# A two-layer trunk step with S5 scan: scan tables and outputs kept on all 128 partitions, quarters of the scan interleaved

## The chip, the cores and the metric

The kernel runs on one core of a Trainium2 chip. The metric is the device time of one execution in microseconds (us), the median of several runs. Less is better.

## The reference

One step of a two-layer trunk over 128 context tokens and 512 latent tokens, all float32, model width 1024. Each layer is

```
h = modulate(x, shift1, scale1); z = h @ w_in
y_a, h_re, h_im = mixer_ssm(u_ssm, ...)      # scan: both directions
y_b = block_attention(q, k, v)               # MLA: q and kv from low-rank parts of z
y_c = mixer_gmlp(uv)
x = x + gate1 * (concat(rms(y_a), rms(y_b), rms(y_c)) * g @ w_out)
x = x + gate2 * conv_ffn(modulate(x, shift2, scale2))
```

and the scan, for each of 16 groups of 16 channels with 64 complex states, forward and reverse, is

```
a_bar = exp(A * dt); b_bar = (a_bar - 1) / A * B
bu    = einsum('gpc,blgc->blgp', b_bar, u)   # edge += a_bar * h0
h     = associative_scan(h = a*h + bu)
y     = einsum('gcp,blgp->blgc', C, h).real  # both directions added, + D * u
y     = gelu(y); y = y * sigmoid(y @ w_glu)
```

The final states of the context tokens (`new_ssm_re`, `new_ssm_im`) are outputs too.

## The kernel before

The scan is chunked: eight time steps become one column of `U` (81 columns `NC`, `NS` = 82 with a start column), so a group's 16 channels by 8 steps fill 128 rows, and a product with a precomputed 128-row table advances eight steps. The 16 groups are handled in four **quarters** of four groups: group `h * 8 + 2 * q + e`, with half `h` and `e` in 0, 1. `ssm_tables` (L530) builds, for each quarter, the tables `we` (input to state), `Q` (state to output) and `tap` (the part of the output that comes straight from the input); `ssm_rotations` (L648) builds the powers `Tr` that turn the complex recurrence into a real one. All go to DRAM (`WEd`, `Qd`, `Wd`, `Td`) and come back per quarter in `ssm_load` (as `we`, `qt`, `tp`, `T`), asked for on the POOL queue. In layer 0, DVE makes the tables of quarters 0 to 2 and POOL those of quarter 3 and the rotations, in front of and beside the input projection; layer 1's tables and rotations are made by POOL during layer 0's ConvFFN.

`ssm_quarter` (L701) does one quarter: 16 products `e` (L716) into two PSUM banks, copies `E` on ACT (L720), start states `h0` and zeros on POOL (L724 to L735), the rotation `m`, `E` on DVE (L744 to L747), the scan `H` (L752), the rotation back (L754, L755), the states `hq` by eight DVE instructions of 64 partitions (L761, L763), twelve products `y` (L775 to L777) into one bank, the copy `ys` (L779) and its way to DRAM (L781). A quarter's matrices hold real parts in rows 0 to 63 and imaginary parts in rows 64 to 127, so each product contracts 128 rows. `ssm_output` (L794) reads `yT` back, does gelu and the `glu` products; then attention begins (`mx`, L1248).

Every tile here has one buffer per tag, so a tile's next load or write waits for its last reader, and one tag may serve two tiles at different times: in layer 0 the rotations' `Tr` uses the memory of `hq`. Two PSUM banks (`pz`) serve `e`, `y` and `tap` in layer 0. The order of the instructions on each engine is not that of the code: a scheduler in the framework sets it when the kernel is built, and each engine then takes its queue strictly in that order. `params` (L166) loads small per-layer vectors; layer 1's are asked for in `mixers` of layer 0, after tables 0 to 2.

## Time and profile before

| | |
|---|---|
| median of 3 runs | 1826.63 us (1825.92 to 1826.67) |
| profiled execution | 1826.58 us, of which its span 1824.8 us and 1.78 us around it |
| TensorE (PE) busy | 1694.3 us, 93% of the span |
| VectorE (DVE) busy | 1156.8 us, 63% |
| ScalarE (ACT) busy | 679.8 us, 37% |
| GpSimd (POOL) busy | 312.8 us, 17% |
| mean granted TensorE clock | 0.95 |

The span of a layer divides into norm, tables and input projection, scan (about 149 to 213 us and 1018 to 1067 us), the rest of the mixers, attention, out projection and ConvFFN. Busy shares are means over stages that differ; the section of rows below gives stretches of 50 us and of 400 us, the waits by engine, and single instructions in order of time. PEclk is the granted clock as a share of full speed.

### The profile page before, as it was taken

To read this page: it belongs to the slowest core of one execution; us is meant where nothing else is said; L and a number is where in the kernel's file an instruction comes from. 1 tells how busy PE (TensorE), PEld (TensorE's weight loads), DVE (VectorE), ACT (ScalarE), POOL (GpSimd) and SP (SyncE) were. 2 spreads that over 40 slices of the span, in tenths; PEclk is the share of its full clock that TensorE was granted. 3 is DMA by queue.
4 is the path that set the end of the run, shared out by engine and by line. 5 is a ranking of instruction groups with operands and counts; after the bars stand their busy time and mean duration, and the time that the engine had idled before them with its cause. 6 is when DMAs were issued, how large, how long until landed. Compare 5 with 4: busy or idle time off the path is not lost.

```text
span 1824.8 us, 28970 instructions
## 1 busy us (share of the span) xinstructions
PE 1694.3 (93%) x11248; PEld 1512.6 (83%) x11248; DVE 1156.8 (63%) x2421; ACT 679.8 (37%) x1210; POOL 312.8 (17%) x738
## 2 busy tenths in 40 slices
PE   5878889999989999999999888999989999999998
PEld 3767755468889999999999876455989999999998
DVE  6887875667674646556477568566786464555564
ACT  4334454433452414224244346343344232332241
POOL 2886200000086060540000120000000000000000
PEclk7889789899899999999999978999989999999999
DMA  9265453301443523234132633540223131331221
GB/s 281 84 174 148 124 162 123 110 15 56 129 137 118 170 56 116 59 94 116 35 90 67 164 105 107 167 133 1 70 70 93 36 104 47 93 92 36 82 82 58
DMA packets 217577, 182.48 MB, mean 100 GB/s; under 512 B 33438, under 2 KB 202204, under 8 KB 217440
## 3 DMA queue, kind: packets, MB, share of 16 engines
q1 hardware_dynamic: 194736, 154.33, 28.2%
q0 software_dynamic: 8272, 23.87, 4.4%
q10 hardware_dynamic: 14432, 2.44, 0.7%
q8 instruction: 89, 1.46, 0.3%
q14 instruction: 48, 0.39, 0.1%
HBM read 161.94 MB, written 18.64 MB: 99 GB/s over the span
## 4 chain that ended last, share of the span: by engine, by line
PE 75%; DVE 10%; DMA 7%; ACT 4%; POOL 2%; issue 2%; ACTq 1%; SPq 0%; DVEq 0%; POOLq 0%
PE up L141 11%; PE up L143 11%; PE up L142 11%; PE dn L142 6%; PE dn L141 6%; PE dn L143 6%; PE o L1287 3%; PE mod L261 2%; DMA raw<-w_mod 2%; PE wo L141 1%; PE wo L143 1%; PE wo L142 1%; DMA raw<-ffn_w_up 1%; PE s L1267 1%; PE win L141 1%
## 5 line engine op out<-in xcount | busy, mean ns | idle before, releaser
L141 PE MATMUL up<-hh,whi 128*128 128x322 f32 x1408 | 435.6, 315 | 8.8 <-ACT hh L357 7.9
L143 PE MATMUL up<-hh,wlo 128*128 128x322 f32 x1408 | 440.9, 314 | 1.1 <-DVE wlo L118 1.0
L142 PE MATMUL up<-hl,whi 128*128 128x322 f32 x1408 | 439.7, 313 | 1.6 <-DVE hl L358 1.5
L141 PEld LDWEIGHTS up<-hh,whi 128*128 128x128 f32 x1408 | 266.1, 191 | 14.3 <-ACT hh L357 7.2
L142 PEld LDWEIGHTS up<-hl,whi 128*128 128x128 f32 x1408 | 268.8, 191 | 2.6 <-DVE hl L358 2.6
L143 PEld LDWEIGHTS up<-hh,wlo 128*128 128x128 f32 x1408 | 267.9, 190 | 2.9 <-DVE wlo L118 1.9
L118 DVE TENSOR_TENSOR wlo<-raw,whi 128x1024 fp32r<-128x1024 f32 (+1 forms) x116 | 146.7, 1266 | 142.2 <-ACT whi L117 141.0
L142 PE MATMUL dn<-glo,dh 128*128 128x322 f32 (+1 forms) x704 | 218.5, 312 | 0.2 <-DVE glo L118 0.2
L143 PE MATMUL dn<-gh,dl 128*128 128x322 f32 (+1 forms) x704 | 217.9, 311 | 0.0
L141 PE MATMUL dn<-gh,dh 128*128 128x322 f32 (+1 forms) x704 | 209.4, 312 | 4.5 <-DVE xT L1501 2.9
L1501 DVE SCALAR_TENSOR_TENSOR xT<-dn,mod,xT 128x320 f32<-128x320 f32 (+2 forms) x288 | 112.2, 435 | 129.5 <-PE dn L143 129.3
L117 ACT CAST whi<-raw 128x1024 fp32r<-128x1024 f32 (+1 forms) x116 | 120.5, 1040 | 151.1 <-PE up L142 56.8
L1532 ACT ACTIVATE cv<-up,prm,cw 128x321 f32<-128x321 f32 x88 | 54.3, 619 | 252.5 <-PE up L143 252.3
L141 PEld LDWEIGHTS dn<-gh,dh 128*128 128x128 f32 x704 | 131.0, 190 | 5.3 <-DVE xT L1501 3.1
L142 PEld LDWEIGHTS dn<-glo,dh 128*128 128x128 f32 x704 | 133.2, 189 | 0.5 <-DVE glo L118 0.5
L143 PEld LDWEIGHTS dn<-gh,dl 128*128 128x128 f32 x704 | 133.5, 190 | 0.0
L1533 DVE SCALAR_TENSOR_TENSOR cv<-up,cw,cv 128x320 f32<-128x320 f32 x88 | 48.3, 549 | 67.5 <-ACT cv L1532 67.5
L261 PE MATMUL mod<-raw,sT 128*32 128x256 f32 x768 | 64.5, 431 | 27.1 <-DMA raw<-w_mod 24.8
L118 DVE TENSOR_TENSOR dl<-raw,dh 128x1024 fp32r<-128x1024 f32 x44 | 54.0, 1227 | 45.8 <-ACT dh L117 45.6
L117 ACT CAST dh<-raw 128x1024 fp32r<-128x1024 f32 x44 | 46.1, 1047 | 56.8 <-DMA raw<-ffn_w_down 50.1
L261 PEld LDWEIGHTS mod<-raw,sT 128*32 128x32 f32 x768 | 19.5, 114 | 57.5 <-DMA raw<-w_mod 29.2
L1250 DVE TENSOR_REDUCE nml<-mx 128x1 f32<-128x640 f32 x64 | 50.9, 820 | 24.0 <-PE mx L1248 23.7
(472 smaller groups left out, 3422.5 us busy)
## 6 DMA issues: line engine op xcount, KB each, us to landing
raw<-w_mod SPq DMA_DIRECT2D x96, 512.0 KB, 4.6
raw<-ffn_w_up SPq DMA_DIRECT2D x88, 512.0 KB, 4.1
raw<-ffn_w_down SPq DMA_DIRECT2D x44, 512.0 KB, 3.5
raw<-w_in SPq DMA_DIRECT2D x10, 512.0 KB, 5.7
we<-WEd POOLq DMA_DIRECT2D x8, 512.0 KB, 4.1
qt<-Qd POOLq DMA_DIRECT2D x8, 512.0 KB, 5.1
raw<-w_out SPq DMA_DIRECT2D x16, 256.0 KB, 5.1
raw<-w_out SPq DMA_DIRECT2D x8, 512.0 KB, 3.4
```

The costliest lines, as they stand in the source:

```text
L117: self.nc.scalar.copy(hi, raw)
L118: self.nc.vector.tensor_tensor(lo, raw, hi.bitcast(F32), op=OP.subtract)
L141: mm(ps, wh, xh, start=start, stop=False)
L142: mm(ps, wh, xl, start=False, stop=False)
L143: mm(ps, wl, xh, start=False, stop=stop)
L261: nc.tensor.matmul(ps[j * 32:j * 32 + 32, c0:c0 + 256], self.sT[:, k0 + j, :], rv[:, j, :], start=k0 == 0, stop=k0 == 4)
L1250: V.tensor_reduce(nm[:, tt:tt + 1], pb[:, :, :320], axis=AX.XY, op=OP.max, negate=True)
L1267: mm(ps, kh[i][:, kc_], qh[i], start=True, stop=False)
L1287: mm(pb[i * 64:(i + 1) * 64, 0], Vt[:, kt, 2 * p + i], Ps[i][kt], start=kt == 0, stop=kt == 4)
L1501: self.nc.vector.scalar_tensor_tensor(self.xT[:, m, a:b], po[:, a - lo:b - lo], self.modcol(l, gi, m, c), self.xT[:, m, a:b], op0=OP.mult, ...
L1532: A.activation(z[:, 0:321], po[:, 0:321], AF.Identity, bias=b, scale=c1)
L1533: V.scalar_tensor_tensor(z[:, 1:321], po[:, 0:320], c0, z[:, 1:321], op0=OP.mult, op1=OP.add)
```

## The change

Scan tables and outputs stay on 128 partitions: the real and the imaginary part of both halves `h` lie in separate columns instead of separate rows. `hq` takes four instructions of 128 partitions in place of eight of 64, `Q` one subtract in place of two, and the copies `bs` go. The products that contracted 128 rows (real over imaginary) become two of 64 rows: `y` is 16 products of 64 rows and 4 of 128 in place of 12 of 128, `tap` 24 of 64 rows in place of 16 of 128, each `h` with its own PSUM bank, evacuated by two copies. The rotations are made in two halves that each serve two quarters in both directions, in layer 0 in the memory of `yA`, no longer of `hq`. The quarters become generators of three steps (load `we` and make `E`; load `T`, `qt`, `tp`; DVE and output), taken in the order 0 0 1 0 1 2 1 2 3 2 3 3. Quarter 0 of layer 1 is no longer loaded ahead of `uT`. The final states leave by eight DMAs a layer in place of two. Layer 1's parameters are asked for on the SP queue.

```diff
 def params(self, l):
+        q = nc.sync if l else nc.gpsimd
...
-                nc.gpsimd.dma_start(out=rows[r0:r1], in_=src)
-            nc.gpsimd.dma_start(out=rows[107:108, :96], in_=I["q_norm"][l:l + 1])
-            nc.gpsimd.dma_start(out=rows[108:109, :96], in_=I["k_norm"][l:l + 1])
+                q.dma_start(out=rows[r0:r1], in_=src)
+            q.dma_start(out=rows[107:108, :96], in_=I["q_norm"][l:l + 1])
+            q.dma_start(out=rows[108:109, :96], in_=I["k_norm"][l:l + 1])
...
+        def tap_of():
+            if not ps_of_:
+                return [self.pz("tap"), self.pz("tap")]
+            pb = self.pb("tap")
+            return [pb[:, 0], pb[:, 1]]
+
...
-        bb = t("bb", [128, 2, 2, 2, 16])
+        bbx = t("bb", [128, 144])
+        nc.gpsimd.memset(bbx[:, 128:], 0.0)
+        bb = bbx[:, :128].rearrange("p (r d g c) -> p r d g c", r=2, d=2, g=2)
...
-
-        bs = t("bs", [128, 2 * 64 + 16])
-        nc.gpsimd.memset(bs[:, 128:], 0.0)
-        for ri in range(2):
-            for h in range(2):
-                nc.scalar.copy(
-                    bs[ri * 64:(ri + 1) * 64, :128].rearrange("p (d h n) -> p d h n", d=2, h=2)[:, :, h],
-                    bb[h * 64:(h + 1) * 64, ri].rearrange("p d g c -> p d (g c)"))
...
-                for h in range(2):
-                    a = slice(h * 64, (h + 1) * 64)
-                    E.tensor_tensor(Q[part * 64:part * 64 + 64, h], tm[0][a], tm[1][a],
-                                    op=OP.subtract)
-            Qv = Q.rearrange("p h (g n) -> p h g n", g=2)
+                E.tensor_tensor(Q[:, part], tm[0], tm[1], op=OP.subtract)
+            Qv = Q.rearrange("p r (g n) -> p r g n", g=2)
...
-            for h in range(2):
-                put.dma_start(out=self.Qd[l][q][:, d, h], in_=Qv[:, h, :, o:o + 128])
+            for part in range(2):
+                put.dma_start(out=self.Qd[l][q][:, d, part], in_=Qv[:, part, :, o:o + 128])
...
-        ps = ps_of("tap")
-        for h in range(2):
-            for e in range(2):
+        ps = tap_of()
+        mm = nc.tensor.matmul
+        for e in range(2):
+            for h in range(2):
...
-                o = ps[gq * 32:gq * 32 + 32, :240]
-                lf = bs[:, gq * 16:gq * 16 + 32]
-                lb = bs[:, 64 + gq * 16:64 + gq * 16 + 32]
-                mm = nc.tensor.matmul
-                mm(o[:, 0:112], lb, Qs[1][:, h, e, 16:128], start=True, stop=True)
-                mm(o[:, 112:128], lb, Qs[1][:, h, e, 128:144], start=True, stop=False)
-                mm(o[:, 112:128], lf, Qs[0][:, h, e, 0:16], start=False, stop=True)
-                mm(o[:, 128:240], lf, Qs[0][:, h, e, 16:128], start=True, stop=True)
+            for o0, o1, d, n0 in ((0, 128, 1, 16), (112, 128, 0, 0), (128, 240, 0, 16)):
+                for r in range(2):
+                    for h in range(2):
+                        a, gq = slice(h * 64, h * 64 + 64), 2 * h + e
+                        c = r * 64 + d * 32 + e * 16
+                        mm(ps[h][gq * 32:gq * 32 + 32, o0:o1], bbx[a, c:c + 32],
+                           Qs[d][a, r, e, n0:n0 + o1 - o0], start=r == 0 and o0 != 112,
+                           stop=r == 1 and o0 != 0)
...
-        nc.scalar.copy(W, ps[:, :240])
+        for h in range(2):
+            nc.scalar.copy(W[h * 64:h * 64 + 64], ps[h][h * 64:h * 64 + 64, :240])
...
-    def ssm_rotations(self, l, pool, E, parts, tags=("Tr", "tr")):
+    def ssm_rotations(self, l, E, homes):
...
-            T = pool.tile([128, N, 2, NS], F32, name=self.uid("Tr"), tag=tags[0], bufs=1)
-            tm = pool.tile([128, 2, N * 32], F32, name=self.uid("tr"), tag=tags[1], bufs=1)
...
+        for a in range(2):
+            T = homes[0][0].tile([128, 2, 4, 2, NS], F32, name=self.uid("Tr"), tag=homes[0][1], bufs=1)
+            tm = homes[1][0].tile([128, 2, 8 * 32], F32, name=self.uid("tr"), tag=homes[1][1], bufs=1)
...
-                sh = [128, N, n]
...
-            for i in range(0, N, 2):
-                d, q = divmod(p0 + i, 8)
-                nc.gpsimd.dma_start(
...
+                sh = [128, 2, 4, n]
+                r_re, r_im = (bc(self.rho[:, j, r, l * 16:l * 16 + 16].rearrange(
+                    "p (d g) -> p d g", d=2)[:, :, 4 * a:4 * a + 4, None], sh) for r in range(2))
...
+            for q in range(2):
+                for d in range(2):
+                    nc.gpsimd.dma_start(
...
+        yield we
...
-        return we, T, qt, tp
-
-    def ssm_quarter(self, l, q, pool, tables, U, st, hq):
+        yield T, qt, tp
+
+    def ssm_quarter(self, l, q, pool, U, st):
...
-        we, T, qt, tp = tables
+        tables = self.ssm_load(l, q, pool)
+        we = next(tables)
...
+        yield
+        T, qt, tp = next(tables)
+        yield
+        hq = t("hq", [128, 2, 2, 2, NS])
+
...
+        for d in range(2):
+            sl = slice(0, 82) if d == 0 else slice(80, None, -1)
+            n = 82 if d == 0 else 81
+            V.tensor_tensor(hq[:, 0, d, :, 0:n], m1[:, d, :, 0, sl], m1[:, d, :, 1, sl],
+                            op=OP.subtract)
+            V.tensor_tensor(hq[:, 1, d, :, 0:n], m2[:, d, :, 0, sl], m2[:, d, :, 1, sl],
+                            op=OP.add)
+        for d in range(2):
+            nc.gpsimd.tensor_copy(st[:, :, d, 2 * q:2 * q + 2], hq[:, :, d, :, 81 if d == 0 else 64])
+        pv = [self.pz("y")[:, :2 * NC].rearrange("p (e k) -> p e k", e=2) for _ in range(2)]
+        for e in range(2):
+            for d in range(2):
+                for r in range(2):
+                    for h in range(2):
+                        a = slice(h * 64, h * 64 + 64)
+                        nc.tensor.matmul(pv[h][:, e], qt[a, d, r, e, :], hq[a, r, d, e, :NC],
+                                         start=d == 0 and r == 0, stop=False)
+            for h in range(2):
+                nc.tensor.matmul(pv[h][:, e], tp[:, h, e], U[:, h * 8 + 2 * q + e, :],
+                                 start=False, stop=True)
+        ys = t("ys", [128, 2, 2, NC])
...
-            a = slice(h * 64, (h + 1) * 64)
-            for d in range(2):
-                sl = slice(0, 82) if d == 0 else slice(80, None, -1)
-                n = 82 if d == 0 else 81
-                V.tensor_tensor(hq[0:64, d, h, :, 0:n], m1[a, d, :, 0, sl], m1[a, d, :, 1, sl],
-                                op=OP.subtract)
-                V.tensor_tensor(hq[64:128, d, h, :, 0:n], m2[a, d, :, 0, sl], m2[a, d, :, 1, sl],
-                                op=OP.add)
-        for d in range(2):
-            c = 81 if d == 0 else 64
-            nc.gpsimd.tensor_copy(
-                st[:, d].rearrange("p (h g) -> p h g", h=2)[:, :, 2 * q:2 * q + 2],
-                hq[:, d, :, :, c])
-        ps = self.pz("y")
-        pv = ps[:, :4 * NC].rearrange("p (h e k) -> p h e k", h=2, e=2)
-        for h in range(2):
-            for e in range(2):
-                o = pv[:, h, e]
-                nc.tensor.matmul(o, tp[:, h, e], U[:, h * 8 + 2 * q + e, :], start=True, stop=False)
-                nc.tensor.matmul(o, qt[:, 0, h, e], hq[:, 0, h, e, :NC], start=False, stop=False)
-                nc.tensor.matmul(o, qt[:, 1, h, e], hq[:, 1, h, e, :NC], start=False, stop=True)
-        ys = t("ys", [128, 2, 2, NC])
-        nc.scalar.copy(ys, pv)
-        for h in range(2):
+            nc.scalar.copy(ys[:, h], pv[h])
...
-        self.tr(ps[:32, :128], st.rearrange("p d g -> p (d g)"))
+        self.tr(ps[:32, :128], st.rearrange("p r d g -> p (r d g)"))
...
-            nc.sync.dma_start(out=self.O[nm][0, l].rearrange("d g p -> (d g) p"),
-                              in_=o[:, ri * 64:(ri + 1) * 64])
+            for d in range(2):
+                for h in range(2):
+                    r = ri * 16 + d * 8
+                    nc.sync.dma_start(out=self.O[nm][0, l, d, h * 8:h * 8 + 8],
+                                      in_=o[r:r + 8, h * 64:(h + 1) * 64])
...
-        yA = mt("yA", [128, 2, NT])
...
-        st = mt("st", [128, 2, 16])
+        st = mt("st", [128, 2, 2, 8])
...
-        tables = self.ssm_load(l, 0, ssm) if l > 0 else None
...
-            self.ssm_rotations(0, ssm, nc.gpsimd, 4, ("hq", "ys"))
-
-        def scans(tables):
-            hq = ssm.tile([128, 2, 2, 2, NS], F32, name=self.uid("hq"), tag="hq")
-            for q in range(4):
-                self.ssm_quarter(l, q, ssm, tables or self.ssm_load(l, q, ssm), U, st, hq)
-                tables = None
+            self.ssm_rotations(0, nc.gpsimd, ((M, "yA"), (ssm, "ys")))
+
+        def scans():
+            steps = [self.ssm_quarter(l, q, ssm, U, st) for q in range(4)]
+            for q in (0, 0, 1, 0, 1, 2, 1, 2, 3, 2, 3, 3):
+                next(steps[q], None)
...
+            yA = mt("yA", [128, 2, NT])
...
+            return yA
...
-            scans(tables)
+            yA = scans()
...
-            scans(None)
+            yA = scans()
```

How that moves the queues is read from the order of the instructions before and after. **PE, layer 0, where the input products of the first quarters stand** (`e` are those products, `win` the input projection, `gm` the gMLP's). Before:

```order
L1110 MATMUL gm_1597<-v_1418,wsT_1563 128x320
L716 MATMUL e_2038<-U_986,we_2029 64x81 x8
L142 MATMUL win_2429<-hl_419,whi_2424 128x320
L143 MATMUL win_2429<-hh_418,wlo_2425 128x320
L141 MATMUL win_2429<-hh_418,whi_2424 128x320
L142 MATMUL win_2429<-hl_419,whi_2424 128x320
L143 MATMUL win_2429<-hh_418,wlo_2425 128x320
L141 MATMUL win_2429<-hh_418,whi_2424 128x320
L1110 MATMUL gm_1602<-v_1418,wsT_1563 128x320
L716 MATMUL e_2049<-U_986,we_2029 64x81 x8
```

After:

```order
L143 MATMUL win_2435<-hh_418,wlo_2431 128x320
L718 MATMUL e_1941<-U_985,we_1938 64x81 x8
L718 MATMUL e_1952<-U_985,we_1938 64x81 x8
L718 MATMUL e_1980<-U_985,we_1977 64x81 x8
L718 MATMUL e_1991<-U_985,we_1977 64x81 x8
L141 MATMUL win_2373<-hh_418,whi_2368 128x322
```

The second quarter's 16 products stood further back, 29 and 65 products of `win` behind the first quarter's; now they follow these at once.

**PE, layer 0, where the first quarter's outputs stand** (`pa` transposes layer 1's parameters). Before:

```order
L142 MATMUL win_2552<-hl_419,whi_2547 128x322
L143 MATMUL win_2552<-hh_418,wlo_2548 128x322
L776 MATMUL y_2088<-hq_2028,qt_2033 128x81
L777 MATMUL y_2088<-hq_2028,qt_2033 128x81
L775 MATMUL y_2088<-U_986,tp_2035 128x81
L776 MATMUL y_2088<-hq_2028,qt_2033 128x81
```

After:

```order
L143 MATMUL win_2373<-hh_418,wlo_2369 128x322
L141 MATMUL win_2435<-hh_418,whi_2430 128x322
L778 MATMUL y_2027<-hq_2010,qt_1973 128x81
L778 MATMUL y_2028<-hq_2010,qt_1973 128x81
L147 MATMUL pa_1912<-ident,rows_1902 128x109
L147 MATMUL pa_1917<-ident,rows_303_1918 128x66
L147 MATMUL pa_1917<-ident,rows_304_1921 128x66
L778 MATMUL y_2027<-hq_2010,qt_1973 128x81
L778 MATMUL y_2028<-hq_2010,qt_1973 128x81
```

Before, 131 products of `win` and 6 of `kv` stood between the first `e` and these outputs; now 25 of `win` stand there. Further on, 20 `win`, 16 `e`, 16 `win`, outputs of quarter 1, 11 `win`, 16 `e`, 6 `kv` and 8 `win` woven with outputs of quarter 2, 16 `win`, outputs of quarter 3; after the last of them stand 30 products of `kv`, before 6.

**SP, layer 0, behind the tables.** Before:

```order
L646 DMA Wd_297<-we_1981 16x8x128 x4
L998 DMA cc_2608<-cache_ckv 128x128
L134 DMA raw_2790<-w_uq 128x768
L258 DMA raw_2940<-w_mod 128x4x256
L258 DMA raw_2946<-w_mod 128x4x256
L781 DMA Yd_305<-ys_2101 128x2x81 x2
```

After:

```order
L646 DMA Wd_297<-we_1890 16x8x128 x4
L184 DMA rows_1902<-b_mod 48x128
L184 DMA rows_1902<-w_out_norm 8x128
L184 DMA rows_1902<-q_a_norm 2x128
L184 DMA rows_1902<-kv_a_norm 1x128
L184 DMA rows_1902<-ffn_conv_b 44x128
L184 DMA rows_1902<-gmlp_b_s 4x128
L185 DMA rows_1902<-q_norm 1x96
L186 DMA rows_1902<-k_norm 1x96
L197 DMA rows_303_1918<-ffn_conv_w 66x128
L197 DMA rows_304_1921<-ffn_conv_w 66x128
L1005 DMA cc_2552<-cache_ckv 128x128
```

Ten parameter loads now stand between the last table and the cache load, and one of the two early loads of `w_mod` has moved behind the first quarter's `Yd`.

## Rows read from the trace of the kernel before

**Rows 1.** The page: the span and the busy times of the engines.

```profile
span 1824.8 us, 28970 instructions
...
PE 1694.3 (93%) x11248; PEld 1512.6 (83%) x11248; DVE 1156.8 (63%) x2421; ACT 679.8 (37%) x1210; POOL 312.8 (17%) x738
```

**Rows 2.** Windows: us, busy us by engine (instructions), granted clock, DMA share.

```profile
100.00:150.00 50.00, 34.29 (x285) 28.95 (x284) 42.06 (x85) 17.57 (x48) 42.12 (x88) 0.83 0.70 189
150.00:200.00 50.00, 42.98 (x339) 38.33 (x339) 39.03 (x97) 21.10 (x50) 23.91 (x67) 0.91 0.47 139
200.00:250.00 50.00, 38.73 (x200) 31.95 (x200) 40.63 (x103) 23.98 (x40) 6.16 (x16) 0.81 0.34 88
...
1000.00:1050.00 50.00, 43.60 (x383) 40.41 (x381) 29.05 (x64) 18.06 (x52) 8.25 (x28) 1.00 0.62 154
...
1050.00:1100.00 50.00, 43.60 (x238) 38.84 (x239) 32.72 (x85) 25.76 (x56) 10.75 (x24) 0.76 0.34 93
...
550.00:950.00 400.00, 400.00 (x2815) 394.21 (x2815) 219.55 (x364) 130.96 (x192) 109.12 (x191) 1.00 0.33 96
```

**Rows 3.** Waits of PE, 60 to 262 us (total, times, longest).

```profile
PE we L147 <- DVE G L95: 13.1, 3, 9.3
PE mod L261 <- DMA raw<-w_mod: 5.2, 4, 2.8
PE y L775 <- DMA tp<-Wd: 3.8, 1, 3.8
```

**Rows 4.** Timeline of DVE, layer 0 scan (start us, us).

```profile
153.34 0.84 DVE L744 TENSOR_TENSOR m<-E,T 128x656 f32<-128x656 f32 x1 [0.75 <-POOL E L727]
...
162.56 1.03 DVE L755 TENSOR_TENSOR m<-H,T 128x656 f32<-128x656 f32 x1
...
175.29 0.32 DVE L761 TENSOR_TENSOR hq<-m 64x164 f32<-64x164 f32 x1 [3.02 <-DMA Td<-Tr]
...
207.84 1.16 DVE L763 TENSOR_TENSOR hq<-m 64x164 f32<-64x164 f32 x4
```

**Rows 5.** Groups by line and form, 60 to 262 us (busy us, mean ns).

```profile
L611 DVE TENSOR_TENSOR Q<-tm,tm 64x288 f32<-64x288 f32 x24 | 13.1, 546 | 0.6
...
L611 POOL TENSOR_TENSOR Q<-tm,tm 64x288 f32<-64x288 f32 x8 | 7.1, 892 | 0.5
```

**Rows 6.** Timeline of POOL and of SP: one DMA request each (start us, us).

```profile
163.65 0.49 POOL L185 DMA_DIRECT2D rows<-k_norm  x1
...
156.96 0.35 SPq L998 DMA_DIRECT2D cc<-cache_ckv  x1
```

**Rows 7.** Waits of PE, 960 to 1135 us.

```profile
PE y L775 <- DMA tp<-Wd: 2.9, 1, 2.9
...
PE y L776 <- DVE hq L763: 2.2, 2, 1.8
...
PE e L716 <- ACT E L720: 1.7, 1, 1.7
...
PE e L716 <- DMA we<-WEd: 1.6, 1, 1.6
```

**Rows 8.** Timeline of PE: outputs y at the two clocks, inputs e.

```profile
178.24 0.39 PE L776 MATMUL y<-hq,qt 128*128 128x81 f32 x2
178.46 0.39 PE L777 MATMUL y<-hq,qt 128*128 128x81 f32 x2
...
202.35 0.63 PE L776 MATMUL y<-hq,qt 128*128 128x81 f32 x2
202.78 0.63 PE L777 MATMUL y<-hq,qt 128*128 128x81 f32 x2
...
1026.09 0.78 PE L716 MATMUL e<-U,we 128*64 128x81 f32 x16
```

**Rows 9.** Timeline of PE in the ConvFFN: one tap group, first and last.

```profile
574.67 0.38 PE L632 MATMUL tap<-Q,bs 128*32 128x112 f32 x2
...
575.85 0.36 PE L635 MATMUL tap<-Q,bs 128*32 128x112 f32 x2
```

28 lines of the change are left out of this document (13 added, 15 removed).

## Prediction

> **What bounds the kernel now.** I read the page first, for where the time can be at all: TensorE is busy for 93% of the span, DVE for 63% [rows 1]. Then I read the windows, since a mean over stages hides their limits. In the ConvFFN TensorE is busy for 400.00 of 400 us at clock 1.00 [rows 2]: nothing that the change does elsewhere can shorten that stage, and every matmul added there is paid. In the four windows around the scans it is not the bound: 34.29, 42.98 and 38.73 busy us in 100 to 250 us, 43.60 and 43.60 in 1000 to 1100 us, at clocks of 0.76 to 1.00 [rows 2]. So TensorE stands idle for 15.7 + 7.0 + 11.3 = 34.0 us around layer 0's tables and scan and for 6.4 + 6.4 = 12.8 us around layer 1's scan. That is nearly all that a change to the scan can win, apart from what the clock gives back: TensorE must do the same products as before, and a shorter scan only lets it do them sooner.
>
> Third, the waits of TensorE name what these idle times hang on: in layer 0 the table products on DVE's `G` for 13.1 us, `mod` on its weights for 5.2 us, `y` on `tp` for 3.8 us [rows 3]; in layer 1 four waits of `y` and `e` of 2.9, 2.2, 1.7 and 1.6 us, 8.4 us together [rows 7]. Last, the timeline of DVE shows why layer 0's scan is late: quarter 0 has rotated back at 163.59 us (162.56 + 1.03), but its first `hq` starts at 175.29 us, released by the DMA `Td<-Tr` [rows 4]. `hq` lies in the memory of the last rotations and must wait until these have left. That is 11.7 us, which DVE fills with other work but for 3.02 us.
>
> **The change part by part.** Durations are from the profiled execution, 1826.58 us, 0.05 us under the median of 1826.63 us.
>
> *Tables, layer 0.* DVE's three tables drop half of the 24 subtracts `Q`, 12 x 0.546 = 6.5 us, POOL's one drops 4 x 0.892 = 3.6 us [rows 5]; a subtract over 128 partitions has the same elements per partition as one over 64, and I take the same time for it. DVE is busy for 42.06 of 50 us in this stretch [rows 2], so much of it is on the path, but DVE has other work to pull forward, and `W` now needs a second copy on ACT. Between 0 and -6.5 us; I take half, -3.
>
> *Scan, layer 0.* The wait for `Td<-Tr` goes: `hq` has its own memory, the rotations that of `yA`. Also `hq` takes four instructions instead of eight. A group of four takes 1.16 us [rows 4], so a quarter saves 1.16 us, four quarters 4.6 us. Quarter 3's `hq` ends at 207.84 + 1.16 = 209.0 us; without the wait and with the shorter `hq` DVE could be there at 209.0 - 11.7 - 4.6 = 192.7 us. The order lets it: the second quarter's `e` follow the first's at once, held in the two PSUM banks until `E` is free, so DVE can go from one quarter's `hq` to the next one's `m` without TensorE between. But these 16.3 us are DVE's, not the kernel's. TensorE is idle for 18.3 us in 150 to 250 us [rows 2], and the waits of `mod` on its weights, 5.2 us [rows 3], come behind the scan and stay: 13.1 us are the ceiling. Some 24 products of `kv` that stood between the scans' products now stand behind them, so little is left to put into the gaps between one quarter's `y` and the next. From 0 to -13; I take -9, near the upper end because the wait that goes is larger than all of it.
>
> *Scan, layer 1.* Of 8.4 us of waits [rows 7], that on `tp` (queued on POOL behind the previous `y`), on `hq` and on `E` are what the interleaving and the shorter `hq` attack, while the load of `we` for quarter 0 is no longer ahead of `uT`. From 0 to -8.4; I take -6.
>
> *Outputs `y`.* A quarter goes from 12 products to 16 + 4. No product of 64 rows stands in this trace, so its price is bounded. One of 128 rows follows the next after 0.22 us (178.24 to 178.46) at full clock and 0.43 us (202.35 to 202.78) at the lower one [rows 8]. If two products on different halves of the rows run side by side, 16 count as 8 and the quarter keeps 12 places: 0. If they don't, 8 places more, 8 x 0.22 = 1.8 us a quarter, 14.4 us for eight quarters. The nearest row is `e`, whose products use 64 columns each: 16 traced matmuls, which are 8 products, in 0.78 us, 0.10 us a product [rows 8], less than half of `y`'s 0.22. Two halves by columns do run side by side; I take rows to do nearly the same and price a quarter at 0.4 us, +3 in all. The Trainium skill, "TensorE: Matmul & The Clock Gate", section on LDWEIGHTS, says that the load of weights takes its time from the number of columns and not from that of the rows; by that alone 20 loads for 12 would give the upper bound.
>
> *Products `tap`.* One table's 16 take 575.85 + 0.36 - 574.67 = 1.54 us [rows 9]. 24 in pairs are 12 places, 24 alone 24 places: -0.4 to +0.8 us each, and a little more for N of 128 instead of 112. The four tables of layer 1 lie where TensorE is never idle. Between -1.6 and +3.2; +1.
>
> *Parameters and small stores.* Ten requests move from POOL, at 0.49 us each, to SP, at 0.35 us [rows 6]: POOL gets 4.9 us back amid the rotations, while on SP the cache load, `w_uq`, one `w_mod` and the `Yd` behind them come up to 3.5 us later. Nothing that TensorE waits for by [rows 3] stands there within that time, so 0; if that cover fails, +3.5. Six more state stores a layer, 6 x 0.35 = 2.1 us on SP, stand ahead of the last `yT`; `glu` now has products of `q` around it, so 0, at worst +2.1 a layer.
>
> The sum: -3 - 9 - 6 + 3 + 1 = -14, and 1826.58 - 14 = 1812.6 us; I forecast 1812.5 us. All gains whole and all costs at nothing would give 1826.58 - 28 = 1798.6 us.
>
> **The rivals.**
>
> *The gain turns into new waits.* In the new order only 25 products of `win` stand between the last `e` and the first `y`, but DVE needs 2 x 0.84 for `m`, the scan and as much again for the way back, 10.3 us from 153.34 to 163.59 us in the trace with other work between [rows 4]. TensorE takes the queue in order, so it would stand at each quarter's `y`, where before work was at hand. Then layer 0 gives -3 and layer 1 -2, tables -3, costs +4: 1822.5 us. For it: two PSUM banks for both `e` and `y`. Against it: what stands behind was idle or slow before too.
>
> *Products of 64 rows are slow.* The slower side, by one mechanism: the pairs don't run side by side. It decides when the costs outweigh the gains of 18 us by 3.7 us (0.2%, about what a measurement of this kernel can tell from no change): with +1 for `tap`, `y` must cost 20.7 us more, 2.6 us a quarter, so 20 products at 0.27 us each and not 0.22. At 0.22 us it is +14.4, and with +3 for `tap` the time is 1826.58 - 18 + 17.4 = 1826 us, no change. At 0.33 us, midway to the lower clock's, a quarter takes 6.6 us for 2.7: +31, 1826.58 - 18 + 31 + 3 = 1842.6 us. Between them 1834 us. For it: `y` and `tap` stand among products of 128 rows, so that the array changes its division four or more times a quarter. Against it: `e` and `mod` change it by columns all the time, and `e` cost little. The Trainium skill, "TensorEngine Tiling (Array Packing)", section Key Properties, says that a change of tiling mode, and not merely of tile, drains TensorE; no trace here shows this by rows, and it speaks for this rival.
>
> *The rotations come too late again.* `T` of quarter 0 is loaded on POOL behind the last table's work, whose memory it shares. POOL has 4.9 + 3.6 us less to do and half as many, longer instructions, so I hold it for unlikely. It would leave tables and layer 1: 1826.58 - 3 - 6 + 4 = 1821.6 us.
>
> **How the numbers follow.** The forecast, a gain of 8 to 20 us, gets 0.50. New waits or late rotations with 3.7 to 8 us of gain get 0.18, more than 20 us 0.09: faster by over 0.2% 0.77. Costs that eat the gain up, as pairs without overlap at 0.22 us, 0.10: within 0.2%. Slow products of 64 rows, 0.13: slower. The range from 1801 to 1828 us leaves out most of the slower case and the last part of the best one, 0.2 together.
>
> **What would show it.** Right: the first `hq` of layer 0 no longer waits for `Td<-Tr` and starts at about 161 us; the last ends before 198 us; `y` of a quarter takes 3.1 us or less at full clock; idle TensorE falls below 26 us in 100 to 250 us and below 9 us in 1000 to 1100 us; the ConvFFN stays within 2 us. Wrong: `y` over 4.5 us a quarter, or `y` waiting on `hq` for over 3 us a quarter, or the granted clock in the scans lower than before.

## The result and the profile after

The change makes the kernel slower: 1840.6 us median of 20 runs (1829.85 to 1851.95) against 1826.65 us of 20 runs before (1823.51 to 1837.92), a ratio of 1.0071 with a 95% interval of 1.0060 to 1.0082, some 13 us. The forecast was 14 us in the other direction, and the range up to 1828 us did not hold it.

The first profiled execution took 1834.06 us, one of the fastest; a second profile of the same kernel (below, the run "after again") took 1840.46 us and stands for the median. The page's span and busy times, first profile, then second; they answer to [rows 1]:

```profile
span 1832.2 us, 29326 instructions
...
PE 1714.5 (94%) x11504; PEld 1524.5 (83%) x11504; DVE 1140.1 (62%) x2377; ACT 675.3 (37%) x1194; POOL 274.6 (15%) x620
```

```profile
span 1838.6 us, 29326 instructions
...
PE 1714.2 (93%) x11504; PEld 1526.2 (83%) x11504; DVE 1143.0 (62%) x2377; ACT 675.6 (37%) x1194; POOL 275.1 (15%) x620
```

Against [rows 1], TensorE's idle time (span less PE busy) fell from 130.5 us to 117.7 and 124.4 us, as the change was meant to do; but its busy time rose from 1694.3 to 1714.5 and 1714.2 us. In the second profile +19.9 us of busy time and -6.1 us of idle time make the +13.8 us of the span. Busy time is not work alone, since a product takes longer at the lower clock: the kernel with the parameters undone, below, has the same products as after and is busy for 1703.9 us. Of the 19.9 us, `tap` covers 8.8 and `y` 7.8 (time in which at least one of its products runs), as told under the prediction's terms; the rest was not taken apart. What the two profiles differ in is told below.

The windows of the second profile, columns as in [rows 2]:

```profile
100.00:150.00 50.00, 40.78 (x346) 34.41 (x345) 37.85 (x80) 14.87 (x40) 35.98 (x53) 0.86 0.74 201
150.00:200.00 50.00, 38.45 (x351) 34.70 (x350) 32.70 (x68) 16.55 (x46) 13.42 (x43) 0.83 0.42 120
200.00:250.00 50.00, 39.26 (x248) 30.15 (x247) 35.45 (x102) 30.09 (x53) 7.96 (x16) 0.90 0.41 117
1000.00:1050.00 50.00, 49.22 (x434) 46.17 (x432) 29.78 (x70) 21.83 (x63) 7.23 (x26) 1.00 0.53 128
1050.00:1100.00 50.00, 42.76 (x266) 38.65 (x266) 27.70 (x57) 18.54 (x45) 9.24 (x26) 0.76 0.45 118
```

TensorE's idle time in 100 to 250 us is 31.5 us, before 34.0: 9.2 for 15.7 us in 100 to 150 us, but 22.3 for 18.3 us in 150 to 250 us. In 1000 to 1100 us it is 8.0, before 12.8. Its waits in layer 0's scan, 145 to 270 us, answer to [rows 3]; that on `tp` is gone, and the waits of `e` on `we` and on `ys` and that of `kv` on `Vt` have come:

```profile
PE e L718 <- DMA we<-WEd: 5.6, 1, 5.6
PE kv L1043 <- ACT Vt L1051: 5.1, 2, 3.2
PE mod L262 <- DMA raw<-w_mod: 3.8, 3, 1.6
PE e L718 <- ACT ys L785: 3.0, 1, 3.0
...
PE y L778 <- DMA qt<-Qd: 1.6, 1, 1.6
```

Where the time goes along the program, from the first start and the last end of each product in the timelines, in us:

| | before | after | after, second |
|---|---|---|---|
| first `e`, layer 0 | 149.06 | 148.17 | 151.35 |
| last `y`, layer 0 | 212.94 | 203.35 | 206.07 |
| first `up`, layer 0 | 456.14 | 459.10 | 460.72 |
| last `dn`, layer 0 | 968.53 | 974.44 | 975.84 |
| first `e`, layer 1 | 1018.77 | 1023.13 | 1027.54 |
| last `y`, layer 1 | 1069.02 | 1073.52 | 1078.95 |
| first `up`, layer 1 | 1335.29 | 1342.15 | 1346.61 |
| span | 1824.8 | 1832.2 | 1838.6 |

The scan of layer 0 ends 7 to 10 us sooner, and all of that is lost again before the ConvFFN begins. The ConvFFN adds 2.7 us, layer 1 up to its own ConvFFN 4 us, and that ConvFFN 2.5 us. Windows from the first `e` to the last `y` of layer 0, and from there to the first `up`, tell why, before and in the second profile:

```profile
149.06:212.94 63.88, 55.99 (x415) 50.15 (x415) 49.47 (x119) 26.63 (x60) 26.94 (x78) 0.87 0.45 131
212.94:456.14 243.20, 219.59 (x1298) 152.81 (x1297) 163.94 (x349) 102.12 (x189) 7.74 (x18) 0.94 0.31 94
```

```profile
151.35:206.07 54.72, 42.50 (x395) 38.53 (x396) 36.23 (x75) 18.49 (x50) 13.83 (x45) 0.84 0.46 134
206.07:460.72 254.65, 229.71 (x1344) 160.81 (x1343) 169.87 (x373) 109.32 (x205) 7.95 (x18) 0.93 0.30 90
```

In the scan TensorE is busy for 13.5 us less and idle for 4.3 us more (12.2 for 7.9); behind it, it is busy for 10.1 us more and idle for 1.3 us more (24.9 for 23.6). So the scan ends sooner because products were moved out of it, not because TensorE waits less, and what was moved is done around it. The DVE timeline of the second profile shows the first `hq` without its wait, against [rows 4], and what came in its place:

```profile
163.15 0.84 DVE L762 TENSOR_TENSOR m<-H,T 128x656 f32<-128x656 f32 x1
...
164.17 0.56 DVE L766 TENSOR_TENSOR hq<-m 128x164 f32<-128x164 f32 x2
...
168.59 0.84 DVE L751 TENSOR_TENSOR m<-E,T 128x656 f32<-128x656 f32 x1 [3.16 <-DMA T<-Td]
...
182.06 0.84 DVE L751 TENSOR_TENSOR m<-E,T 128x656 f32<-128x656 f32 x1 [4.96 <-DMA T<-Td]
...
193.88 0.84 DVE L751 TENSOR_TENSOR m<-E,T 128x656 f32<-128x656 f32 x1 [3.01 <-DMA T<-Td]
...
200.00 0.56 DVE L768 TENSOR_TENSOR hq<-m 128x164 f32<-128x164 f32 x2
```

`hq` begins at 164.17 us, 0.18 us behind the way back, where it began at 175.29 us before. But DVE then stands 3.16, 4.96 and 3.01 us ahead of the three next `m`, each time for `T`. Quarter 3 is through at 200.56 us.

### The profile page after: what moved, and what is told of

Read it like the earlier page. It is cut to its first block, busy times and chain, and to the rows that moved or that the text cites. A ratio compares the mean times of both kernels' runs of the same rounds, so it can differ in the third digit from the quotient of the medians.

```text
span 1832.2 us, 29326 instructions
## 1 busy us (share of the span) xinstructions
PE 1714.5 (94%) x11504; PEld 1524.5 (83%) x11504; DVE 1140.1 (62%) x2377; ACT 675.3 (37%) x1194; POOL 274.6 (15%) x620
## 4 chain that ended last, share of the span: by engine, by line
PE 73%; DVE 10%; DMA 8%; ACT 4%; issue 2%; POOL 1%; ACTq 0%; SPq 0%; DVEq 0%; POOLq 0%
PE up L141 11%; PE up L143 11%; PE up L142 11%; PE dn L141 5%; PE dn L142 5%; PE dn L143 5%; PE o L1294 3%; PE mod L262 2%; PE wo L141 1%; DMA T<-Td 1%; DMA raw<-w_mod 1%; PE wo L143 1%; PE wo L142 1%; PE s L1274 1%; PE tap L632 1%
## 5 line engine op out<-in xcount | busy, mean ns | idle before, releaser
L141 PE MATMUL up<-hh,whi 128*128 128x322 f32 x1408 | 436.6, 315 | 10.1 <-ACT hh L358 4.2
L143 PEld LDWEIGHTS dn<-gh,dl 128*128 128x128 f32 x704 | 133.4, 190 | 0.6 <-DVE dl L118 0.6
```

Source lines behind the costliest of these rows:

```text
L141: mm(ps, wh, xh, start=start, stop=False)
L143: mm(ps, wl, xh, start=False, stop=stop)
```

## The experiments

The edits are to the kernel before or after as named. Each kernel's order is made anew by the scheduler, so no edit changes one thing alone. Busy and idle are TensorE's, from the page of the profiled execution, which is up to 10 us off the median of its kernel. Ratios are to runs of before on the same chip, where before's median is 1826.65 to 1830.97 us; so rows are compared by their ratios.

| run | median us | ratio, 95% interval | span | busy | idle |
|---|---|---|---|---|---|
| before | 1826.65 | | 1824.8 | 1694.3 | 130.5 |
| after, second profile | 1840.46 (one run) | 1.0071, 1.0060 to 1.0082 (the 20 runs) | 1838.6 | 1714.2 | 124.4 |
| layout alone | 1857.64 | 1.0151, 1.0118 to 1.0183 | 1856.1 | 1709.0 | 147.1 |
| interleaving alone | 1831.23 | 1.0005, 0.9984 to 1.0025 | 1826.6 | 1689.2 | 137.4 |
| rotations alone | 1839.22 | 1.0046, 1.0023 to 1.0070 | 1842.2 | 1699.8 | 142.4 |
| after, tap over four columns | 1843.47 | 1.0084, 1.0065 to 1.0103 | 1842.1 | 1708.7 | 133.4 |
| after, two buffers of `we` | 1855.46 | 1.0144, 1.0121 to 1.0166 | 1854.2 | 1715.9 | 138.3 |
| after, rotations undone | 1834.50 | 1.0035, 1.0014 to 1.0055 | 1838.2 | 1710.8 | 127.4 |
| after, parameters undone | 1839.55 | 1.0070, 1.0044 to 1.0097 | 1834.3 | 1703.9 | 130.4 |
| after, rotations undone, tap over four | 1824.04 | 0.9970, 0.9956 to 0.9985 | 1827.6 | 1703.6 | 124.0 |
| after, `y` one half at a time | 1846.85 | 1.0082, 1.0052 to 1.0111 | 1846.1 | 1714.0 | 132.1 |
| interleaving and parameters alone | 1829.54 | 0.9993, 0.9976 to 1.0011 | 1831.3 | 1687.6 | 143.7 |
| layout, interleaving, tap over four | 1837.33 | 1.0042, 1.0023 to 1.0061 | 1825.4 | 1702.5 | 122.9 |

**The layout alone.** After, with interleaving, rotations and parameters as before:

```diff
-            for q in (0, 0, 1, 0, 1, 2, 1, 2, 3, 2, 3, 3):
-                next(steps[q], None)
+            for q in range(4):
+                for _ in self.ssm_quarter(l, q, ssm, U, st):
+                    pass
```

> The kernel after with everything undone but the layout: tables, Q, tap, hq, y and state stores on 128 partitions; quarters one after the other, rotations in four parts in the memory of hq, parameters on POOL. Theory 1 (the 64-row products are the loss): 8 to 14 us slower than before, from tap at about 3.4 us a table where it was 1.54 us (four of them in the ConvFFN, where TensorE is never idle, +7.5 us) and from y at 3.3 us a quarter where it was 2.7. Theory 2 (the new order of the quarters is the loss): within 4 us of before, as tap's excess is offset by DVE's shorter tables and hq.

Twice theory 1's upper price: +27 us. Busy time grew by 14.7 us, about what the products take more (`tap` covers 8.5 us more than before, `y` 6.3); idle time grew by 16.6 us, which theory 1 didn't have. `y` now takes both PSUM banks, so the next quarter's `e` can only follow the last quarter's `y` and its copies; the last `e` of layer 0 ends at 221 us (before 200), the last `y` at 237 us (before 213). The gelu behind it is late, and TensorE waits in layer 0's scan and after it:

```profile
PE glu L832 <- ACT gl L827: 16.0, 2, 13.3
PE win L141 <- ACT sqk L993: 9.7, 1, 9.7
```

So the interleaving, which puts two quarters' `e` ahead of the first `y`, is what makes the layout bearable (with it and the new parameters, the kernel with the rotations undone below, the ratio is 1.0035). Neither part can be priced without the other.

**The interleaving alone**, before with the generators and their order (`hq` as a tile of its own):

```diff
+            steps = [self.ssm_quarter(l, q, ssm, U, st) for q in range(4)]
+            for q in (0, 0, 1, 0, 1, 2, 1, 2, 3, 2, 3, 3):
+                next(steps[q], None)
```

> The kernel before with one part of the change, the interleaved quarters (order 0 0 1 0 1 2 1 2 3 2 3 3, no early load for layer 1). Theory 1: within 4 us of before or faster by up to 5. Theory 2: 5 to 12 us slower, with a wait of about 4.5 us of the second quarter's e on its load of we, and waits of kv on ACT behind the scan of layer 0.

No difference clear of the interval, -3 to +5 us. Theory 2 as stated falls: no cost of reordering alone shows, and the wait on `we` is 0.5 us here.

**The rotations alone**, before with the new `ssm_rotations` in both layers; the call in layer 0:

```diff
-            self.ssm_rotations(0, ssm, nc.gpsimd, 4, ("hq", "ys"))
+            self.ssm_rotations(0, nc.gpsimd, ((M, "yA"), (ssm, "ys")))
```

> The kernel before with one part of the change, the rotations in two halves in the memory of yA. Both theories: the first hq of layer 0 no longer waits for Td<-Tr and starts about 10 us sooner. If that wait bounded anything, 3 to 9 us faster; if TensorE has the same work to do anyway, within 3 us of before.

8 us slower, which neither theory expected. DVE's timeline, layer 0:

```profile
166.77 0.84 DVE L755 TENSOR_TENSOR m<-H,T 128x656 f32<-128x656 f32 x1
...
167.79 1.14 DVE L761 TENSOR_TENSOR hq<-m 64x164 f32<-64x164 f32 x4
...
209.21 0.84 DVE L744 TENSOR_TENSOR m<-E,T 128x656 f32<-128x656 f32 x1 [3.99 <-POOL E L727]
```

The first `hq` does start 7.5 us sooner than in [rows 4], so the wait that the prediction read as 11.7 us is gone. But the last quarter's `m` starts at 209.21 us, before 201.01 us, behind 3.99 us of waiting for POOL, and the first `e` at 153.32 us, before 149.06 us. A long wait that goes in front of an order made anew bought nothing.

**After again**, the kernel after unchanged.

> The kernel after once more, for a second profile: the first profile stands 6.5 us under the median of the runs. Theory 3 (the granted clock makes the difference): a profile near 1840 us shows more time at the lower clock, above all in the first 100 us, where the first profile shows 1.00 and that of before 0.71 and 0.92. Otherwise the difference lies in waits, and the sum of the clock lost is as in the first.

There is more time at the lower clock, as theory 3 said: the granted clock in the first 100 us is 1.00 in the first profile and 0.83 in the second. The loss there (busy time times one less the clock, summed over stretches of 10 us) is 10.6 us of full-speed work in the second, before 12.3; over the whole span the first profile loses 64 us, the second 76, before 68. But that the clock makes the 6.4 us between the two spans is not shown: TensorE is busy for 1714.5 and 1714.2 us, and what differs is its idle time, 117.7 and 124.4 us. The first profile, 7.4 us over before, shows too little of the loss.

**Tap over four columns.** After, with the groups `e` inside:

```diff
-        for e in range(2):
-            for h in range(2):
...
-            for o0, o1, d, n0 in ((0, 128, 1, 16), (112, 128, 0, 0), (128, 240, 0, 16)):
-                for r in range(2):
-                    for h in range(2):
+        for o0, o1, d, n0 in ((0, 128, 1, 16), (112, 128, 0, 0), (128, 240, 0, 16)):
+            for r in range(2):
+                for e in range(2):
+                    for h in range(2):
```

> The kernel after with the tap products in another order: e is the innermost loop but one, so that four neighbours lie on four column groups and both halves of the rows. If tap's 3.4 us a table come from too little running side by side, a table falls to 1.6 to 2.2 us, the ConvFFN of layer 0 loses 5 to 7 us of TensorE's time, and the whole is 4 to 9 us faster than after (about 1833 us where after has 1840). If the price is one of 64-row products as such, it stays at 3.4 us and the time within 3 us of after.

One table's two runs of `tap` in the ConvFFN, the first of them, after (second profile, with the product behind it) and here:

```profile
663.48 1.72 PE L632 MATMUL tap<-Q,bb 64*32 64x128 f32 x24
665.13 0.41 PE L141 MATMUL up<-hh,whi 128*128 128x322 f32 x1
```

```profile
673.47 1.14 PE L633 MATMUL tap<-Q,bb 64*32 64x128 f32 x24
```

A table falls from 2 x 1.72 to 2 x 1.14 us, so the price is not one of 64 rows as such. In after the 24 records of such a run start one after another for the most part, here two by two: here the products run side by side, in after most of them did not. Busy time falls by 5.5 us. Yet the time, which was to fall by 4 to 9 us, does not (1.0084 for 1.0071), since idle time rises by 9.0 us, 7.6 of them in the first 90 us of layer 0's ConvFFN; the last section tells what stands there.

**Two buffers of `we`**, after with a tag of its own for odd quarters.

```diff
-        we = t("we", [128, 2, 2, 2, 128])
+        we = t("we1" if q % 2 else "we", [128, 2, 2, 2, 128])
```

> The kernel after with a second buffer for we, odd quarters in their own. If the wait of e on the load of we (4.5 and 5.6 us in the two profiles of after) delays the scan of layer 0, it goes and layer 0 ends 3 to 6 us sooner; if e was early anyway, the wait moves to y on hq and the time is within 2 us of after.

A miss on both sides: some 13 us slower than after (1.0144 for 1.0071). The wait on `we` is gone, but another stands in front of the first `y`, where the parameters' transposes were put:

```profile
PE pa L147 <- DMA rows<-ffn_conv_w: 6.0, 1, 6.0
```

Its first `e` is at 157.30 us, 6 us later than in the second profile of after, with more idle time (34.6 for 28.5 us) and a lower clock (0.70 for 0.83) in the first 100 us. Why these came is not settled.

**The rotations undone**, after with `ssm_rotations` of before in both layers (in layer 0 four parts, memory of `hq`).

> The kernel after with the rotations as before, in four parts in the memory of hq. By the run with the rotations alone (1.0046 of before) it is 4 to 10 us faster than after, with e of layer 0 some 2 to 4 us sooner and the first hq waiting for Td<-Tr again. If the parts don't add up, because the order is made anew each time, within 3 us of after or slower.

6 us faster, as the run alone had said. The first `e` is at 144.51 us and `up` begins at 454.27 us, 6.4 us sooner than in the second profile of after. In the profiled execution, 5.6 us over the median, the ConvFFN loses that again: it is 8 us longer, by the same idle time as with tap over four columns. One thing expected did not come: the first `hq` does not wait for `Td<-Tr`. It starts at 161.52 us, 0.9 us behind the way back, since POOL has done the last rotation at 156.11 us; in before that was at 171.34 us. So the wait of before hung on when POOL ends the rotations, and the shared memory alone does not bring it back.

**The parameters undone**, after with

```diff
-        q = nc.sync if l else nc.gpsimd
+        q = nc.gpsimd
```

> The kernel after with layer 1's parameters asked for on POOL as before. The prediction held this part for 0: within 3 us of after. If the requests in SP's queue delay the loads behind them, 3 to 6 us faster.

1.0070 against 1.0071: here the part is worth nothing that shows, as predicted.

**Rotations undone and tap over four columns**, both edits of above.

> The kernel after with the rotations as before and the tap products over four column groups, both parts that showed less work or an earlier scan. TensorE's busy time falls by about 6 us against after (1714 us) to 1705 to 1709 us; if its idle time stays near 124 us, the time is 5 to 9 us below after (1831 to 1835 us). If the ledger of busy and idle time doesn't hold, because the order made anew adds idle time as in the runs before, 1836 to 1845 us.

Both came out under the range: the busy time at 1703.6 us, and the time at 1824.04 us, 5 us faster than before. It is the one version that beats both, called the fast version below. Against the second profile of after TensorE is busy for 10.6 us less at equal idle time; `tap` covers 17.1 us for 23.2, which is 6.1 of them.

**`y` one half at a time**, after with the loop over `h` outside, so that in each run of eight products four on one half stand ahead of four on the other:

```diff
-            for d in range(2):
-                for r in range(2):
-                    for h in range(2):
+            for h in range(2):
+                for d in range(2):
+                    for r in range(2):
```

> The kernel after with the 64-row products of y in another order: all eight of a pair of groups on the upper half of the rows first, then those on the lower half, so that neighbours lie on the same rows. If the two halves run side by side in after (0.26 us a pair), the eight products of a run take 0.2 us and more each, a quarter 4.4 to 5.4 us at full clock where after has 3.3, TensorE is busy for 8 to 16 us more and the time is 5 to 15 us above after. If they don't, a quarter stays at 3.3 us and the time within 3 us of after.

One quarter of layer 0 here at full clock, to hold against the next section's of after (x16 are 8 products):

```profile
177.38 1.63 PE L778 MATMUL y<-hq,qt 64*128 64x81 f32 x16
178.94 0.67 PE L781 MATMUL y<-U,tp 128*128 128x81 f32 x4
179.55 1.63 PE L778 MATMUL y<-hq,qt 64*128 64x81 f32 x16
181.11 0.67 PE L781 MATMUL y<-U,tp 128*128 128x81 f32 x4
```

Eight products so ordered take 1.56 us up to the next start, 0.20 us each; in after, in pairs, 1.05 us, 0.13 each. So the halves do run side by side where they alternate, and an unpaired product of 64 rows costs little less than one of 128 (0.22). The quarter is 4.40 us long, and `y` covers 45.5 us for 37.0 in both layers. But TensorE's busy time as a whole is 1714.0 us, no more than after's, where 8 to 16 us more were expected, and 1.0082 is not told apart from after's 1.0071. The profile's 7.7 us of added idle time stand in the first 90 us of layer 0's ConvFFN (13.0 for 5.3 us), where `dn` waits for 9.0 us as the last section tells; they are not the price of `y`.

**Interleaving and parameters alone**, before with both.

> The kernel before with the two parts of the change that add no product: the interleaved quarters and the parameters on SP, without the layout and without the new rotations. TensorE's busy time stays at 1689 to 1696 us. If the products are the loss, within 4 us of before, and faster by 2 to 6 us if the interleaving shortens idle time in both layers.

Within 4 us of before: 0.9993. TensorE was busy for 6.7 us less than before, with the same products, and stood idle for 13 us more; with old rotations and old products no gain of the interleaving shows.

**Layout, interleaving, tap over four columns**, the fast version with the parameters on POOL.

> The kernel after with the rotations and the parameters as before and the tap products over four column groups: layout and interleaving alone. In its order only 24 products of q and none of kv stand between the last y and attention in layer 0, and the rotations of layer 1 stand where the layout alone had them. If the waits that decide are the products of kv behind the scan and DVE's 8.6 us wlo beside POOL's rotations at the start of layer 0's ConvFFN (a wait of dn of 9.3 us), both are absent, TensorE is busy for 1700 to 1706 us, idle for under 122 us, and the time is 2 to 8 us below the run with the rotations undone and tap over four columns (1824 us). If other waits take their place, 1822 to 1830 us.

A miss: 1837.33 us, and 1.0042 where the fast version has 0.9970, by the line of the parameters alone. Both named waits are absent and the busy time is as said (idle time 122.9 us), but the scan itself ended late, last `y` at 219.91 us, and `glu` took the place of what went:

```profile
PE glu L833 <- ACT gl L828: 10.4, 2, 7.5
```

**The same kernel twice more.** Its profile stood 10 us under its own median.

> The kernel of e12 once more, for a second profile: the first (1827.2 us) stands 10 us under the median of its 12 runs. If the granted clock makes the difference, as between the two profiles of after, a profile near 1837 us has the same order and waits at the start, and more time at the lower clock in named stretches. If DVE and POOL in each other's way make it, an instruction of DVE of several us beside POOL stands in a stretch where the first profile has none.

> The same kernel a third time, since one of two profiles may again be a fast one. Same expectation as the run before.

1830.27 and 1830.71 us, busy 1700.6 and 1700.8, idle 127.8 and 128.1 us. The clock explains no difference here: the third has a good start (about 1 us lost in 100 us, the second 10.7) and is no faster. These two ran on another chip, where one run of before took 1821.72 us; on that of the 12 runs before's median is 1830.97 us. By that one run their ratios are 1.0047 and 1.0049, close to the 1.0042 of the 12, so that 1830 and 1837 us may be one and the same here. What made the first profile shorter was not caught; that stays open. The account of after rests on its second profile, which is at the median.

**One edit in two kernels.** Some edits were made twice, and each has another worth in another order. Tap over four columns: nothing that shows in after (1.0071 to 1.0084), some 12 us with the rotations undone (1.0035 to 0.9970). Rotations undone: 6 us in after, some 21 us with tap over four columns (1.0084 to 0.9970). Parameters on POOL: nothing in after, 13 us slower in the fast version. So a difference of 10 us between two orders says little about the edit behind it; prices read from the products themselves, in us a table or a quarter, say more.

## Why the prediction was wrong

**The frame was right, its sizes were not, and with them the sign.** It said that only TensorE's idle time could be won and that added work is paid. Idle time fell by 6.1 us where 18 were taken, busy time rose by 19.9 us where 4 were taken. By the windows of [rows 2] idle time went down by 6.5 us in 100 to 150 us ("Tables", 3 taken) and by 4.8 us in 1000 to 1100 us ("Scan, layer 1", 6 taken), but up by 4.0 us in 150 to 250 us ("Scan, layer 0", 9 taken). The steps that failed are the pairs, which `tap` and `y` were priced by and which the queue often did not have, the clock of `y`, and the gain of layer 0's scan. "Tables" won more idle time than taken, but TensorE is busy for 7 us more up to the first `e`, which is 2.3 us later.

**"Products `tap`", +1, was mis-sized most.** I counted between 12 places (24 products in pairs) and 24 (alone) against the old 16, at the old 0.10 us a product, and for the four tables of layer 1 only. But the old 0.10 us was already the price of products that run side by side. In one table before, the next column group's first product (L632) has its record between those of the last product of the group ahead (L635), 0.04 to 0.06 us apart where each lasts 0.26 us:

```profile
575.57 0.26 PE L635 MATMUL tap<-Q,bs 128*32 128x112 f32 x1
575.63 0.26 PE L632 MATMUL tap<-Q,bs 128*32 128x112 f32 x1
575.67 0.26 PE L635 MATMUL tap<-Q,bs 128*32 128x112 f32 x1
```

After takes 3.4 us for two of the four tables in the ConvFFN, 0.14 us a product, and 2.3 and 2.1 us for the two others. In the first two the records start one after another for the most part, as told above: these products are not in pairs. Summed over the stretches that `tap` covers, 14.5 us before are 23.2 us after, 8.8 more: 5.2 for the four tables of layer 1 in the ConvFFN, where TensorE is hardly ever idle and the upper bound was 3.2, and 3.6 in layer 0, which the term left out. The rule that I should have used is that a product's price is read with its neighbours: the run with four columns, where a table costs 2.3 us twice and 1.7 and 1.6 us for the others, got 6.5 us back (16.8 us).

**"Outputs `y`", +3.** The price of pairs at full clock was nearly right. One quarter of layer 0, second profile, four lines of 8, 2, 8 and 2 products:

```profile
202.69 1.12 PE L778 MATMUL y<-hq,qt 64*128 64x81 f32 x16 [1.62 <-DMA qt<-Qd]
203.74 0.67 PE L781 MATMUL y<-U,tp 128*128 128x81 f32 x4
204.34 1.12 PE L778 MATMUL y<-hq,qt 64*128 64x81 f32 x16
205.40 0.67 PE L781 MATMUL y<-U,tp 128*128 128x81 f32 x4
```

That is 3.38 us from 202.69 to 206.07, where 2.7 were and 3.1 forecast. The Trainium skill, "TensorE: Matmul & The Clock Gate", section on LDWEIGHTS, has the load of weights go by columns and not by rows, which gave the upper bound of 4.5 us; the runs deny that bound in pairs and nearly grant it without (4.40 us). What the term missed is seen in layer 1, where a quarter looks like this,

```profile
1060.48 3.33 PE L778 MATMUL y<-hq,qt 64*128 64x81 f32 x16 [0.84 <-ACT vsq L1125]
1063.74 1.14 PE L781 MATMUL y<-U,tp 128*128 128x81 f32 x4
1064.81 2.00 PE L778 MATMUL y<-hq,qt 64*128 64x81 f32 x16
1066.74 1.14 PE L781 MATMUL y<-U,tp 128*128 128x81 f32 x4
```

7.4 us at the lower clock, where before had one of four quarters there in 4.98 us. Both runs of eight are at the same clock (0.50), yet the first takes 3.33 us and the second 2.00. In the second two records start together every 0.21 us, in the first nearly each starts alone: its products are not in pairs. In layer 0 such a run stands at full clock, as long as those with `y` one half at a time:

```profile
179.76 1.63 PE L778 MATMUL y<-hq,qt 64*128 64x81 f32 x16
```

By the starts of the records, 5 of the 16 runs of eight products in this profile are not in pairs, 3 of them in layer 1, and they take about 5 us more than pairs would. The code alternates the halves; that the scheduler's order undid it is inferred from the starts. Over both layers `y` covers 29.2 us before and 37.0 after: +7.8, of which 7.1 in layer 1. Part of these is the clock and not the new products: with the interleaving alone the old `y` covers 17.1 us in layer 1 for before's 14.4, 46 of its 96 records at the lower clock for 22.

**"Scan, layer 0", -9.** The wait for `Td<-Tr` went, as said, and `hq` halved. But TensorE did not get the 9 us: idle time in 150 to 250 us rose from 18.3 to 22.3 us. Two steps failed. First, DVE did not run from one `hq` to the next `m`: I had looked at PSUM and `E`, and not at `T`, whose one buffer is free only after the way back and for whose load DVE then stood 3.0 to 5.0 us, 11.1 us in three quarters, nearly the 11.7 us that went. (Of those 11.7 us DVE stood for 6.3 in all, also for `whi` and others, and not for 3.02 alone.) Second, the cost that I named and then left out of the sum: 24 products of `kv` moved behind the scan. The way from the last `y` to the first `up` of layer 0 can be held across the runs against the number of `kv` products on it:

| `kv` behind the last `y` | runs | us to `up` |
|---|---|---|
| 0 | rotations alone; layout alone; layout, interleaving, tap over four | 240.2; 234.0; 235.0 (238.0 and 239.6 in its other two profiles) |
| 6 | before; interleaving alone | 243.2; 239.8 |
| 18 | parameters undone; interleaving and parameters | 243.6; 243.5 |
| 24 | rotations undone; the same with tap over four | 247.1; 244.5 |
| 30 | after, twice; tap over four; two `we`; `y` one half | 255.8, 254.7; 255.1; 253.6; 253.7 |

All five with 30 are 6 us and more above the others (in the three with none, part of `q` is ahead of the last `y` as well). In after that is mostly moved work and not a new wait: `kv` covers 9.0 us behind the last `y`, before 1.5, and idle time there is 24.9 us for 23.6. The waits on `Vt` of 5.1 us above stand beside others that are gone, such as that of `q` on `hsq`, 3.4 us before. This is seen across orders and was not tried by itself.

**"Scan, layer 1", -6.** The waits of [rows 7] shrank and idle time in 1000 to 1100 us fell by 4.8 us, not far from the 6 taken; `y` at 7.1 us more took that and more.

**Rotations too late again**, held for unlikely, is the nearest to what the runs with and without them show: +8 us alone, -6 us when undone. The reason given (POOL has less to do) was true, POOL is busy for 275 us and not 313, and beside the point: the time went by where the scheduler put them and what else moved with them, which these runs don't take apart further.

**Parameters, 0**, was right for this kernel; in the fast version the same line is worth 13 us. The slower rival had the right end. Its mechanism, pairs that don't run side by side, holds in 5 of 16 runs of `y` and in two of four tables of `tap` in the ConvFFN, and not in the others. Of the test points, in the second profile, the first `hq` lost its wait (164.2 us, about 161 was said) and idle time in 1000 to 1100 us was 8.0 us (under 9); the others failed: `y` 3.38 us (3.1), idle time in 100 to 250 us 31.5 us (26), the ConvFFN +2.7 us (2), the last `hq` at 200.6 us (198).

The Trainium skill, "TensorEngine Tiling (Array Packing)", section Key Properties, has it that a change of mode drains TensorE. The first `up` behind other products does have a longer step: behind the tap of 64 rows above, `up` starts at 665.13 us and its next at 665.38; neighbours of `up` otherwise follow after 0.15 us. But behind the transposes `we`, 128x128 like `up` itself, it is nearly the same: `up` starts at 567.18 us and its next at 567.41. So these rows show no price of a change of mode.

## What to carry to other kernels

Price a replaced matmul by the places it holds among its neighbours, at both clocks, and not by counting instructions: sixteen 32-column products already shared the array, and the split by rows, in its first order, cut that sharing. Pairs in the code need not be pairs in the queue: look whether two records start together. Ask of every buffer in a loop that is to be interleaved when it is free again, above all the ones that DMAs fill; a wait that goes shows the next one of its size. Where a scheduler orders the queues, count what moved behind the critical stretch, for that work will be done there; a stretch that ends sooner may only hold less.

## What the runs showed of the hardware

A DVE instruction with both inputs in SBUF can stand until POOL, which works without a pause, is done. In layer 0's ConvFFN of the fast version, DVE (start, us), then POOL at the same time (some of the rotations' instructions, which follow each other without a gap), then TensorE's wait there:

```profile
526.57 1.22 DVE L118 TENSOR_TENSOR dl<-raw,dh 128x1024 fp32r<-128x1024 f32 x1
...
530.15 0.55 DVE L1543 SCALAR_TENSOR_TENSOR cv<-up,cw,cv 128x321 f32<-128x321 f32 x1
532.99 8.63 DVE L118 TENSOR_TENSOR wlo<-raw,whi 128x1024 fp32r<-128x1024 f32 x1 [2.28 <-ACT whi L117]
```

```profile
526.43 0.21 POOL L91 TENSOR_TENSOR Tr<-Tr,rho 128x16 f32<-128x16 f32 x1
526.61 1.25 POOL L93 TENSOR_TENSOR Tr<-Tr,rho 128x16 f32<-128x16 f32 x1
...
533.03 0.40 POOL L92 TENSOR_TENSOR tr<-Tr,rho 128x128 f32<-128x128 f32 x1
...
540.08 0.45 POOL L96 TENSOR_TENSOR Tr<-Tr,tr 128x144 f32<-128x144 f32 x1
```

```profile
PE dn L141 <- DVE cv L1549: 9.3, 1, 9.3
```

`wlo` is an instruction of 1.27 us in the mean of the page before, and took 8.63 us: it ends 1.1 us after POOL's last, at 540.53 us. The `cv` of 320 columns, which read one input from PSUM, keep their 0.55 us beside the same POOL. It goes the other way too: `dl` at 526.57 us, also with both inputs in SBUF, takes its usual 1.22 us amid POOL's run, and POOL's instruction of 526.61 us takes 1.25 us where the one ahead of it, of the same size, takes 0.21. Why `dl` got its turn there and `wlo` did not is not shown. `dn` waits 9.3 us for `wlo`, by way of the `cv` behind it, here, with the rotations undone and with tap over four columns; in before the longest `wlo` of this ConvFFN is 3.29 us, in the second profile of after 2.81, so it is no part of after's loss. The Trainium skill, "SBUF — State Buffer", section "SBUF: two separate sides", says that the two engines lock a shared port for a whole instruction. The 1.25 us of POOL's instruction agree with that; but `wlo` got no turn between POOL's instructions, none of which took over 0.72 us, only when the run of them stopped. This is most of what took back the gain of the tap over four columns (7.6 of 9.0 us of idle time), and it is still in the fast version.
